# The first projection unit makes values, queries and keys together, and the squares of x leave GpSimd

## The chip, the cores and the metric

The kernel runs on one core of one Trainium2 chip. The metric is the device time of one execution in microseconds (us). The core has five engines, each with a queue of its own that is worked off in a fixed order: TensorE (PE, matmuls; PEld is its weight loads), VectorE (DVE), ScalarE (ACT), GpSimd (POOL) and SyncE (SP), which here only starts the DMAs. Waits between engines go over semaphores.

## What is computed

One decoder layer on 256 positions of width 1024, all in fp32:

```
hn  = rmsnorm(h, g_attn[i])
qkv = hn @ w_in[i]                       # (256, 3072)
qa, ka, va = split_heads(qkv[..., :1536], 8)
qb, kb, vb = split_heads(qkv[..., 1536:], 8)
ya = rmsnorm(merge_heads(dilated_mixture(qa, ka, va, slopes_a)), g_out_a[i])
yb = rmsnorm(merge_heads(moba_attention(qb, kb, vb, slopes_b)), g_out_b[i])
h = h + concat([ya, yb]) @ w_out[i]
hn = rmsnorm(h, g_mlp[i])
h = h + square(relu(hn @ w_up[i])) @ w_down[i]
gate = sigmoid(rmsnorm(h, g_ple[i]) @ w_ple_gate[i] + b_ple_gate[i])
h = h + gate * (p[i] @ w_ple_proj[i])
out = rmsnorm(h, g_final)
```

At 256 positions both attentions become plain causal attention with a bias table per head (a distance penalty; in group A also the logarithm of how many of the three dilated branches see a key).

## The kernel before

Every fp32 matrix product is made of three matmuls in a rounded format: the function `mm3` (L151 to L155) multiplies high by high, high by low and low by high halves. So every weight slab and x itself are first split: ScalarE rounds the tile to its high half (`hi`, L75, or `xhi`, L219) and VectorE subtracts to get the low half (`lo`, L76, or `xlo`, L220). x is kept transposed, as eight row blocks of 128 features by 256 tokens. The norm of x is not applied ahead of the projection but behind it: the squares of x are summed (`xsq`, L245 to L254), a matmul with ones gives the sums per token (`x_stats`), and the reciprocal root scales values (`v_evac`), queries and keys (`evac_qk`, by way of `x_bcast`, which spreads it over the partitions as `rb`).

The work is a list of units. A unit has slabs of weights (1 MB each, four row blocks by 512 columns) and a generator of steps; one step is one `mm3`. `run_units` (L109) loads the slabs two units ahead, splits the next unit's slabs in pieces while the steps of this unit run, and calls the functions that the unit's table `inserts` names after a given number of steps. The units of the projection are: values of group A (16 steps of two times 512 columns' worth of tokens by columns), then queries and keys of head pairs 0 and 1 (32 steps of 256 columns), of pairs 2 and 3, the same two for group B, and values of group B. The attention of a head pair is cut into functions that are inserted there: `E_` scales q and k and splits them, `B_` builds the bias on GpSimd, `S_` makes the scores, their softmax and, on GpSimd at L337, the normalised probabilities `pb`, `T_` transposes `pb` on TensorE (L347), `V_` multiplies with the values. With two bias buffers, `B_` of a pair waits until the scores of the pair two ahead have read theirs; on GpSimd it stands ahead of the `pb` steps of the pair before.

The first unit is special. Its loads are cut into single row blocks of 128x512 (256 KB; the first one in halves), with x between them, in groups of blocks `(0, 1), (1, 2), (2, 4), (4, 6), (6, 8)`; the first block of x comes with the gains in one tensor `head` (147 KB). All of its splitting, and the squares on GpSimd, are issued ahead of its matmuls:

```
for k0, k1 in groups:
    if k0 == 0:
        x_split(k0, k1)
        ...
    else:
        ps[k0]()
        x_split(k0, k1)
    for k in range(k0 + 1, k1):
        ps[k]()
    x_squares(k0, k1)
```

The rest of the kernel (output projection, MLP, gate, final norm) follows as further units.

## Time and profile before

| | us |
|---|---|
| timed runs | 351.67, 349.98, 351.51; median 351.51 |
| the profiled execution | 348.54 |
| its span, first to last instruction | 346.8 |
| PE busy | 331.6 (96%) |
| DVE busy | 221.6 (64%) |
| ACT busy | 198.3 (57%) |
| POOL busy | 91.0 (26%) |
| mean granted clock of TensorE | 0.989 |

The profiled execution is one run, 1.7 us longer than its span, and 3.0 us shorter than the median of the timed ones. The busy share of an engine is a mean over the whole span. TensorE has two clock levels, 1.2 and 2.4 GHz; the granted clock of a stretch is the mean share of the higher one. The ends of matmuls in a profile are modelled; their starts are recorded.

### The profile page before, as it was taken

The numbers are of one execution on the slowest core, as the hardware profiler recorded it, in microseconds if no ns is written. First come the engines' busy times: TensorE is split into PE (matmuls) and PEld (weight loads), VectorE is DVE, ScalarE is ACT, GpSimd is POOL, SyncE is SP. The second block draws the span as 40 slices with busy tenths as digits, with TensorE's granted clock in tenths as the row PEclk, the third lists the DMA queues.
The fourth block names the chain that finished last, engine by engine and source line by source line (L and its number), as shares of the span: only waits on it lengthen the run. The fifth ranks groups of instructions, "written<-read, shape, count | busy, mean of one in ns | idle before, by whom it ended". The sixth has DMA issues, their size and how long they took to land.

```text
span 346.8 us, 5629 instructions
## 1 busy us (share of the span) xinstructions
PE 331.6 (96%) x2188; PEld 296.6 (86%) x2188; DVE 221.6 (64%) x371; ACT 198.3 (57%) x370; POOL 91.0 (26%) x120
## 2 busy tenths in 40 slices
PE   7899999999989999999999999999999999999990
PEld 6689889999866889898998988989989899888890
DVE  4898999786855669637537275293553843757563
ACT  5676667785783668738345374372652825458431
POOL 1887574554222001311010110110201102000443
PEclk9899999999999999999999999999999999999997
DMA  6996844435264078563737618356194472700011
GB/s 180 370 381 227 316 160 135 159 123 194 94 241 154 15 241 315 200 231 106 259 124 239 246 38 327 124 169 259 58 322 163 133 246 107 242 2 0 2 61 61
DMA packets 10827, 60.87 MB, mean 176 GB/s; under 512 B 1200, under 2 KB 1968, under 8 KB 4016
## 3 DMA queue, kind: packets, MB, share of 16 engines
q1 hardware_dynamic: 10800, 60.51, 49.5%
q8 instruction: 17, 0.28, 0.3%
q14 instruction: 10, 0.08, 0.1%
HBM read 59.46 MB, written 1.05 MB: 174 GB/s over the span
## 4 chain that ended last, share of the span: by engine, by line
PE 81%; POOL 7%; DVE 5%; ACT 2%; issue 2%; DMA 2%; SPq 1%; POOLq 0%; DVEq 0%; ACTq 0%
PE ps L153 26%; PE ps L154 25%; PE ps L155 25%; DVE lo L76 3%; POOL xsq L254 2%; POOL pb L337 2%; DMA xT<-in_xT 2%; POOL sq L253 1%; PE ps L359 1%; PE ps L316 1%; PE ps L347 1%; ACT pb L331 1%; PE ps L476 1%; PE ps L360 1%; SPq L212 0%
## 5 line engine op out<-in xcount | busy, mean ns | idle before, releaser
L76 DVE SCALAR_TENSOR_TENSOR lo<-raw,head,hi 128x512 fp32r<-128x512 f32 (+2 forms) x137 | 109.8, 851 | 24.3 <-ACT hi L75 24.2
L75 ACT ACTIVATE hi<-raw,head 128x512 fp32r<-128x512 f32 (+2 forms) x137 | 92.6, 734 | 26.0 <-PE ps L154 11.2
L153 PE MATMUL ps<-hhi,hi 128*128 128x256 f32 x256 | 72.6, 283 | 0.0
L155 PE MATMUL ps<-hhi,lo 128*128 128x256 f32 x256 | 72.4, 283 | 0.0
L154 PE MATMUL ps<-hlo,hi 128*128 128x256 f32 x256 | 72.4, 283 | 0.0
L84 DVE TENSOR_TENSOR lo<-raw,hi 128x1024 fp32r<-128x1024 f32 x34 | 41.5, 1254 | 28.1 <-ACT hi L83 28.0
L540 POOL TENSOR_TENSOR sq<-r 128x512 f32<-128x512 f32 (+1 forms) x18 | 19.9, 1107 | 141.8 <-ACT r L538 141.8
L153 PE MATMUL ps<-hi,u 128*128 128x512 f32 x128 | 50.2, 392 | 0.0
L83 ACT ACTIVATE hi<-raw 128x1024 fp32r<-128x1024 f32 x34 | 34.3, 1052 | 27.2 <-PE ps L155 25.5
L154 PE MATMUL ps<-lo,u 128*128 128x512 f32 x128 | 49.9, 390 | 0.0
L155 PE MATMUL ps<-hi,u 128*128 128x512 f32 x128 | 49.8, 389 | 0.0
L153 PEld LDWEIGHTS ps<-hhi,hi 128*128 128x128 f32 x256 | 49.1, 192 | 0.3
L154 PEld LDWEIGHTS ps<-hlo,hi 128*128 128x128 f32 x256 | 49.1, 192 | 0.3
L155 PEld LDWEIGHTS ps<-hhi,lo 128*128 128x128 f32 x256 | 49.1, 192 | 0.0
L153 PE MATMUL ps<-xhi,hi 128*128 128x256 f32 x128 | 37.8, 297 | 0.0
L154 PE MATMUL ps<-xlo,hi 128*128 128x256 f32 x128 | 36.0, 282 | 0.0
L155 PE MATMUL ps<-xhi,lo 128*128 128x256 f32 x128 | 35.4, 282 | 0.0
L543 DVE TENSOR_TENSOR u<-sq,u 128x512 fp32r<-128x512 f32 (+1 forms) x18 | 11.7, 651 | 34.0 <-ACT u L542 34.0
L155 PEld LDWEIGHTS ps<-hi,u 128*128 128x128 f32 x128 | 24.0, 188 | 5.0
L153 PEld LDWEIGHTS ps<-hi,u 128*128 128x128 f32 x128 | 24.1, 188 | 4.7
L154 PEld LDWEIGHTS ps<-lo,u 128*128 128x128 f32 x128 | 24.1, 188 | 4.7
L153 PEld LDWEIGHTS ps<-xhi,hi 128*128 128x128 f32 x128 | 24.4, 191 | 1.2 <-issue 0.7
(128 smaller groups left out, 540.2 us busy)
## 6 DMA issues: line engine op xcount, KB each, us to landing
raw<-in_w_up SPq DMA_DIRECT2D x16, 1024.0 KB, 5.0
raw<-in_w_down SPq DMA_DIRECT2D x16, 1024.0 KB, 4.8
raw<-in_w_in SPq DMA_DIRECT2D x10, 1024.0 KB, 6.3
raw<-in_w_out SPq DMA_DIRECT2D x4, 1024.0 KB, 4.8
raw<-in_w_gate SPq DMA_DIRECT2D x4, 1024.0 KB, 4.9
raw<-in_w_in SPq DMA_DIRECT2D x7, 256.0 KB, 6.7
h_sb<-in_x SPq DMA_DIRECT2D x1, 1024.0 KB, 7.2
raw<-in_w_ple SPq DMA_DIRECT2D x1, 1024.0 KB, 4.9
```

What stands on the lines that cost most here:

```text
L75: nc.scalar.activation(h, r, AF.Copy, scale=sc)
L76: nc.vector.scalar_tensor_tensor(l, r, sc, h.bitcast(F32), op0=ALU.mult, op1=ALU.subtract)
L83: nc.scalar.activation(h, r, AF.Copy)
L84: nc.vector.tensor_tensor(l, r, h.bitcast(F32), op=ALU.subtract)
L153: nc.tensor.matmul(ps, lhs[0], rhs[0], start=start, stop=False)
L154: nc.tensor.matmul(ps, lhs[0], rhs[1], start=False, stop=False)
L155: last_mm[0] = nc.tensor.matmul(ps, lhs[1], rhs[0], start=False, stop=stop)
L253: nc.gpsimd.tensor_tensor(sq, x, x, op=ALU.mult)
L254: nc.gpsimd.tensor_tensor(xsq, xsq, sq, op=ALU.add)
L337: nc.gpsimd.tensor_scalar(pb[:, h, sl], pb[:, h, sl], nm[:, 2, c], 1.0, op0=ALU.mult, op1=ALU.mult)
L540: nc.gpsimd.tensor_tensor(sq, r, r, op=ALU.mult)
L543: nc.vector.tensor_tensor(o[1], sq, o[0].bitcast(F32), op=ALU.subtract)
```

## The change

The first unit now makes the values of group A and the queries and keys of head pairs 0 and 1, one row block of x after the other: for each block two steps of values, then four of q/k. It holds six accumulators at once. The loads are put in the order in which the blocks need them. The next unit's pieces begin after 33 of its 48 steps (`idle`). The squares of x are made on ScalarE and added on VectorE, and the scaled identity of `x_stats` is made on VectorE. The tables of inserts are rewritten: q and k of both pairs are finished at the end of the first unit and the start of the next, and scores, transposes and values of the later pairs move against the steps. The diff, cut to its core:

```diff
@@ run_units
-        ps = [p for s in units[0].slabs for p in s.pieces()]
-        for k0, k1 in groups:
...
+        v, qk = ([p for s in slabs_in[u] for p in s.pieces()] for u in range(2))
+        for k in range(KT):
+            if k in (0, 1, 2, 4):
+                x_split(k, k + (1 if k < 2 else 2))
+            for col in halves if k == 0 else [slice(None)]:
+                v[k](cols=col)
+            qk[k]()
+            if k == 4:
+                x_split(6, 8)
+            if k:
+                x_squares({1: range(2), 2: range(2, 4), 4: range(4, 6), 5: range(6, 8)}.get(k, ()))
...
-                want = min(len(todo), math.ceil(len(todo) * (j + 1) / (0.8 * u.n)))
+                want = min(len(todo), math.ceil(len(todo) * max(j + 1 - u.idle, 0) / (0.8 * (u.n - u.idle))))
@@ loads
+    for col in halves:
+        block_load(0, 0, 1, col)
+    block_load(1, 0, 1)
+    x_load(1, 2)
+    for u in range(2):
+        block_load(u, 1, 2)
+    x_load(2, 4)
+    for k in (2, 3):
+        for u in range(2):
+            block_load(u, k, k + 1)
+    x_load(4, 8)
+    for k in (4, 6):
+        for u in range(2):
+            block_load(u, k, k + 2)
@@ first_loads
-        slabs_in[1][0].load()
         nc.sync.dma_start(ident, a["consts"][:, 3 * S :])
-        slabs_in[1][1].load()
+        slabs_in[2][0].load()
         nc.sync.dma_start(consts[:, : 2 * S], a["consts"][:, : 2 * S])
+        slabs_in[2][1].load()
@@ x_squares
-                nc.gpsimd.tensor_tensor(sq, x, x, op=ALU.mult)
-                nc.gpsimd.tensor_tensor(xsq, xsq, sq, op=ALU.add)
+                nc.scalar.activation(sq, x, AF.Square)
+                nc.vector.tensor_tensor(xsq, xsq, sq, op=ALU.add)
@@ x_stats
-            nc.gpsimd.tensor_scalar(diag[:, t], ident, xr["r"][:, t : t + 1], 1.0, op0=ALU.mult, op1=ALU.mult)
+            iv = nc.vector.tensor_scalar(diag[:, t], ident, xr["r"][:, t : t + 1], None, op0=ALU.mult)
@@ the new first unit, and two lines of its table and the next one's
+    def first_steps():
+        tiles = []
+        for k in range(KT):
...
+                for t in range(2):
+                    v_step(0, 0, k, t)
+                    yield
+            s = slabs_in[1][k // 4]
+            for c in range(4):
...
+                mm3(tiles[c][:, :S], (s.hi[:, k % 4, col], s.lo[:, k % 4, col]), (aT[0][:, k], aT[1][:, k]),
+                    k == 0, k == KT - 1)
...
+                yield
...
+             {33: [x_stats], 42: [x_bcast], 46: [VE(0), B_(0, 0)], 48: [E_(0, 0)]}, 60, 33),
...
+             {3: [E_(0, 1)], 8: [S_(0, 0), B_(0, 1), late_loads], 16: [E_(0, 2)], 22: [S_(0, 1), B_(0, 2)],
+              24: [T_(0, 0)], 30: [V_(0, 0)]}, 32),
```

The first place where instructions stand anew is ScalarE at the start of the program. In the names, `raw_111` and `raw_112` are the values' two slabs, `raw_113` and `raw_114` the q/k slabs of the first two pairs (before, `raw_138` and `raw_141`), `xT_108` is x. Before, the rows from the first high half on were:

```order
L219 ACTIVATE xhi_109<-head_67 128x256
L75 ACTIVATE hi_146<-raw_111,head_67 128x256 x2
L75 ACTIVATE hi_146<-raw_111,head_67 128x512
L219 ACTIVATE xhi_109<-xT_108 128x256
L75 ACTIVATE hi_146<-raw_111,head_67 128x512
L219 ACTIVATE xhi_109<-xT_108 128x512
L75 ACTIVATE hi_146<-raw_111,head_67 128x512
L75 ACTIVATE hi_172<-raw_112,head_67 128x512
```

Now the same place reads:

```order
L230 ACTIVATE xhi_109<-head_67 128x256
L261 ACTIVATE xsq_138<-head_67 128x256
L75 ACTIVATE hi_151<-raw_111,head_67 128x256 x2
L75 ACTIVATE hi_157<-raw_113,head_67 128x512
L230 ACTIVATE xhi_109<-xT_108 128x256
L264 ACTIVATE sq_168<-xT_108 128x256
L75 ACTIVATE hi_151<-raw_111,head_67 128x512
L75 ACTIVATE hi_157<-raw_113,head_67 128x512
L230 ACTIVATE xhi_109<-xT_108 128x512
L264 ACTIVATE sq_177<-xT_108 128x256
L75 ACTIVATE hi_151<-raw_111,head_67 128x512
```

Values and q/k blocks alternate, and a square stands behind each high half of x.

The second place is VectorE from q and k of pair 0 to the scores of pair 0 (the operations at L322 and L325, now L334 and L337, two for each head). Before:

```order
L287 TENSOR_TENSOR q_361<-ps4_283,rb_132 128x256
L288 SCALAR_TENSOR_TENSOR k_362<-ps5_291,rb_132 128x256
L76 SCALAR_TENSOR_TENSOR lo_288<-raw_198,head_67,hi_287 128x512 x4
L292 TENSOR_TENSOR q_366<-q_361,q_365 128x256
L294 TENSOR_TENSOR k_368<-k_362,k_367 128x256
L76 SCALAR_TENSOR_TENSOR lo_349<-raw_200,head_67,hi_348 128x512 x4
L287 TENSOR_TENSOR q_473<-ps8_378,rb_132 128x256
L322 ISA sc_445,nm_447<-ps10_431,bias_373 128x256
```

Now:

```order
L299 TENSOR_TENSOR q_419<-ps4_242,rb_137 128x256
L300 SCALAR_TENSOR_TENSOR k_420<-ps5_246,rb_137 128x256
L299 TENSOR_TENSOR q_454<-ps6_250,rb_137 128x256
L76 SCALAR_TENSOR_TENSOR lo_395<-raw_147,head_67,hi_394 128x512 x2
L304 TENSOR_TENSOR q_424<-q_419,q_423 128x256
L306 TENSOR_TENSOR k_426<-k_420,k_425 128x256
L76 SCALAR_TENSOR_TENSOR lo_395<-raw_147,head_67,hi_394 128x512 x2
L76 SCALAR_TENSOR_TENSOR lo_444<-raw_223,head_67,hi_443 128x512
L300 SCALAR_TENSOR_TENSOR k_455<-ps7_254,rb_137 128x256
L304 TENSOR_TENSOR q_459<-q_454,q_458 128x256
L334 ISA sc_499,nm_501<-ps12_485,bias_406 128x256
```

q and k of pair 1 (`q_454`, `k_455`) have come between those of pair 0 and the first scores; the low halves between are five instead of eight, and two more follow between the two heads' scores.

## Rows read from the trace of the kernel before

**Rows 1.** The page's part 1, TensorE: busy us, share, instructions.

```profile
PE 331.6 (96%) x2188; PEld 296.6 (86%) x2188; DVE 221.6 (64%) x371; ACT 198.3 (57%) x370; POOL 91.0 (26%) x120
```

**Rows 2.** Waits of TensorE, 0 to 55 us: us in total, times, longest.

```profile
PE ps L153 <- ACT xhi L219: 2.4, 2, 1.8
PE ps L347 <- POOL pb L337: 1.5, 2, 1.1
...
PE ps L260 <- POOL xsq L254: 0.8, 1, 0.8
```

**Rows 3.** The same from 56 to 110 us.

```profile
PE ps L347 <- POOL pb L337: 1.2, 1, 1.2
```

**Rows 4.** Stretches: us, busy (count) of each engine, granted clock, DMA share, GB/s.

```profile
6.00:8.00 2.00, 1.40 (x7) 1.05 (x6) 1.35 (x2) 1.09 (x2) 0.85 (x1) 1.00 0.68 173
...
10.00:12.00 2.00, 1.77 (x6) 1.17 (x7) 1.88 (x2) 1.54 (x3) 1.92 (x4) 0.90 0.90 281
12.00:14.00 2.00, 2.00 (x6) 1.52 (x5) 2.00 (x3) 1.63 (x3) 2.00 (x3) 0.50 1.11 434
14.00:16.00 2.00, 2.00 (x8) 1.62 (x7) 2.00 (x3) 1.70 (x3) 1.92 (x2) 0.75 0.98 405
```

**Rows 5.** Timeline of ScalarE, 2 to 20 us: start, us, operation [idle before].

```profile
5.11 0.72 ACT L75 ACTIVATE hi<-raw,head 128x512 fp32r<-128x512 f32 x1 [0.68 <-DMA raw<-in_w_in]
6.20 0.42 ACT L219 ACTIVATE xhi<-xT 128x256 fp32r<-128x256 f32 x1 [0.36 <-DMA xT<-in_xT]
7.33 0.73 ACT L75 ACTIVATE hi<-raw,head 128x512 fp32r<-128x512 f32 x1 [0.71 <-DMA raw<-in_w_in]
9.46 0.63 ACT L219 ACTIVATE xhi<-xT 128x512 fp32r<-128x512 f32 x1 [1.41 <-DMA xT<-in_xT]
...
11.20 0.72 ACT L75 ACTIVATE hi<-raw,head 128x512 fp32r<-128x512 f32 x1 [0.28 <-DMA raw<-in_w_in]
12.33 0.63 ACT L219 ACTIVATE xhi<-xT 128x512 fp32r<-128x512 f32 x1 [0.40 <-DMA xT<-in_xT]
...
17.57 2.56 ACT L75 ACTIVATE hi<-raw,head 128x512 fp32r<-128x512 f32 x4 [1.83 <-DMA raw<-in_w_in]
```

**Rows 6.** Timeline of VectorE, 3 to 36 us.

```profile
14.46 2.36 DVE L76 SCALAR_TENSOR_TENSOR lo<-raw,head,hi 128x512 fp32r<-128x512 f32 x2
...
28.44 0.42 DVE L287 TENSOR_TENSOR q<-ps,rb 128x256 f32<-128x256 f32 x1 [0.65 <-PE ps L155]
...
33.77 2.73 DVE L76 SCALAR_TENSOR_TENSOR lo<-raw,head,hi 128x512 fp32r<-128x512 f32 x4
```

**Rows 7.** Timeline of TensorE: two paces, first scores, first transposes.

```profile
19.74 0.39 PE L153 MATMUL ps<-hi,xhi 128*128 128x512 f32 x1
...
19.97 0.39 PE L154 MATMUL ps<-lo,xhi 128*128 128x512 f32 x1
...
34.09 0.91 PE L316 MATMUL ps<-k,q 64*128 64x256 f32 x12
...
35.26 0.28 PE L155 MATMUL ps<-xhi,lo 128*128 128x256 f32 x1
35.38 0.28 PE L153 MATMUL ps<-xhi,hi 128*128 128x256 f32 x1
...
44.04 0.55 PE L347 MATMUL ps<-ident,pb 128*128 128x128 f32 x3 [1.11 <-POOL pb L337]
```

**Rows 8.** Timeline of GpSimd, 26 to 46 us.

```profile
38.02 0.94 POOL L304 TENSOR_SCALAR bias<-consts 128x256 f32<-128x256 f32 x2 [4.80 <-DVE nm L325]
...
40.65 3.34 POOL L337 TENSOR_SCALAR pb<-pb,nm 128x256 f32<-128x256 f32 x4
```

**Rows 9.** Groups of GpSimd, 2 to 30 us: count, busy us, mean ns.

```profile
L254 POOL TENSOR_TENSOR xsq<-xsq,sq 128x256 f32<-128x256 f32 x7 | 7.3, 1049 | 0.3
```

**Rows 10.** Groups of VectorE, 30 to 110 us.

```profile
L322 DVE CUSTOM_DVE_ANT_0 sc<-ps,bias 128x256 f32<-128x256 f32 x16 | 6.7, 417 | 3.0 <-PE ps L316 2.9
L325 DVE CUSTOM_DVE_ANT_0 sc<-ps,bias 128x128 f32<-128x128 f32 x16 | 4.5, 283 | 0.0
```

More of the change, by code (lines that the diff above doesn't have):

```diff
@@ L88, in block_kernel, with __init__ @@
     class Unit:
-        def __init__(self, slabs, steps, inserts=None, n=None):
-            self.slabs, self.steps, self.inserts, self.n = slabs, steps, inserts or {}, n
+        def __init__(self, slabs, steps, inserts=None, n=None, idle=0):
+            self.slabs, self.steps, self.inserts, self.n, self.idle = slabs, steps, inserts or {}, n, idle
     later = []
@@ L110, in run_units @@
         first_loads()
[L111 to L122 removed]
+        v, qk = ([p for s in slabs_in[u] for p in s.pieces()] for u in range(2))
[9 more added lines that the diff above has]
+                x_squares({1: range(2), 2: range(2, 4), 4: range(4, 6), 5: range(6, 8)}.get(k, ()))
         for i, u in enumerate(units):
[L124 to L126 removed]
+            for s in units[i + 2].slabs if i + 2 < len(units) else []:
+                s.load()
             todo = [p for s in (units[i + 1].slabs if i + 1 < len(units) else []) for p in s.pieces()]
@@ L406, in v_evac, with v_step @@
         for t in range(2):
-            nc.scalar.activation(vt[g][:, t], held[g][t], AF.Copy, scale=xr["r"][:, t : t + 1])
+            ia = nc.scalar.activation(vt[g][:, t], held[g][t], AF.Copy, scale=xr["r"][:, t : t + 1])
+        first.append(ia)
+    def v_step(u, g, k, t):
+        if k == t == 0:
+            vt[g] = ap.tile([P, 2, 512], F32, tag="vt", name="vt", bufs=2)
+            held[g] = [bank() for _ in range(2)]
+        s = slabs_in[u][k // 4]
+        tok = slice(t * P, (t + 1) * P)
+        mm3(held[g][t], (aT[0][:, k, tok], aT[1][:, k, tok]), (s.hi[:, k % 4], s.lo[:, k % 4]),
+            k == 0, k == KT - 1)
@@ L409, in v_steps @@
     def v_steps(u, g):
         def steps():
-            vt[g] = ap.tile([P, 2, 512], F32, tag="vt", name="vt", bufs=2)
-            ps = [bank() for _ in range(2)]
             for k in range(KT):
-                s = slabs_in[u][k // 4]
-                parts = halves if u == 0 and k == 0 else [slice(0, 512)]
-                for col in parts:
+                for t in range(2):
+                    v_step(u, g, k, t)
+                    yield
+        return steps
+    def first_steps():
+        tiles = []
+        for k in range(KT):
+            if k == 0:
+                vt[0] = ap.tile([P, 2, 512], F32, tag="vt", name="vt", bufs=2)
+                held[0] = [bank() for _ in range(2)]
+                s = slabs_in[0][0]
+                for col in halves:
@@ L417, in steps @@
                     for t in range(2):
                         tok = slice(t * P, (t + 1) * P)
-                        mm3(ps[t][:, col], (aT[0][:, k, tok], aT[1][:, k, tok]),
-                            (s.hi[:, k % 4, col], s.lo[:, k % 4, col]), k == 0 and col == parts[0], k == KT - 1)
-                        if col == parts[-1]:
-                            yield
-            held[g] = ps
-        return steps
+                        mm3(held[0][t][:, col], (aT[0][:, 0, tok], aT[1][:, 0, tok]),
+                            (s.hi[:, 0, col], s.lo[:, 0, col]), not col.start, False)
@@ new lines, in first_steps @@
+                yield
+                yield
+            else:
+                for t in range(2):
+                    v_step(0, 0, k, t)
+                    yield
+            s = slabs_in[1][k // 4]
+            for c in range(4):
+                if k == 0:
+                    tiles.append(bank())
+                col = slice(c * P, (c + 1) * P)
+                mm3(tiles[c][:, :S], (s.hi[:, k % 4, col], s.lo[:, k % 4, col]), (aT[0][:, k], aT[1][:, k]),
+                    k == 0, k == KT - 1)
+                if k == KT - 1 and c % 2:
+                    qk_ps[0, c // 2] = tiles[c - 1], tiles[c]
+                yield
```

54 lines of the change are left out of this document (17 added, 37 removed).

## The prediction, on record before the run

> **What bounds the kernel now.** I read the busy shares first. TensorE is busy for 331.6 of the 346.8 us of the span [rows 1], so only time in which TensorE stands or runs slowly can be won, and the change issues the same projection matmuls as before. Then I read what TensorE waited for. In the first 55 us it waited 2.4 us for the high halves of x, 1.5 us for the normalised probabilities `pb` and 0.8 us for `xsq`, the sum of squares [rows 2]; later, up to 110 us, there is one wait worth naming, 1.2 us, again for `pb` [rows 3]. The stage table adds a loss that no wait shows: the granted clock is 0.90, 0.50 and 0.75 in the three stretches from 10 to 16 us [rows 4], so 0.4, 2.0 and 1.0 us passed at 1.2 GHz instead of 2.4, which halves 3.4 us of work and costs 1.7 us. Before it fell TensorE had been busy for 1.40 us of the 2 us from 6 to 8 [rows 4] and had then stood for 1.8 us at a stretch [rows 2]. So the place is the front of the kernel: 2.4 + 1.7 + 0.8 us in the two units that the change merges, and 1.5 us at the first transposes.
>
> **The paces.** A dense 512-column matmul starts every 0.23 us, a 256-column one every 0.12 us [rows 7]. A row block of x is 6 of the first kind for the values (1.37 us) and 12 of the second for two head pairs (1.44), together 2.81 us; eight of them are 22.5 us. ScalarE makes a high half of 128x512 in 0.72 us, or every 0.61 us back to back (2.56 us for 4), and a 128x256 pass in 0.42 (0.36 back to back) [rows 5]. VectorE makes a low half in 1.18 us while GpSimd works on squares, and in 0.68 while GpSimd stands still [rows 6]: 33.77 lies in a gap of GpSimd, which begins its next work at 38.02 [rows 8].
>
> **Arrivals.** ScalarE's starts after a DMA wait tell when each place of the queue has landed. Counting bytes in the queue's order, 671 KB are there at 5.1, 1065 at 7.3, 1327 at 9.4, 1851 at 11.2, 2113 at 12.3 and 4211 at 17.5 us [rows 5]; the last stretch is 400 KB per us. The new queue has other tensors at the same places and begins with seven DMAs of the same sizes. So I take the same clock for the same byte. Then the first block of q/k weights is there at 5.1, values block 1 at 7.3, q/k block 1 at 9.4, x blocks 2 and 3 at 10.3, values block 2 at 11.2, q/k block 2 at 12.3, block 3 by 13.6, x blocks 4 to 7 at 14.9, the rest between 16.2 and 20.1, the next unit's two slabs at 22.9 and 26.2.
>
> **The first unit, block by block.** Each block waits for landing + 0.73 (high half) and then + 0.75 (low half).
> Values block 0: the square of x now stands between the high half of x and that of the weights on ScalarE, so it starts 0.3 us later, at 4.4, and ends at 6.1. Q/k block 0 runs at once, to 7.5. Values block 1: high half 8.05, so 0.55 us idle; low half 8.84, another 0.35; ends 9.8. Q/k block 1: high half 10.2, low half 11.0, 0.4 and 0.55 idle; ends 12.2. Values block 2: low half 12.7, 0.3 idle; ends 13.9. From there the halves are ready before TensorE is: block 3's q/k low half at 15.2 against 16.7, values block 4's at 18.3 against 18.4. Five blocks and a half at 2.81, plus 0.6 us each for the two small statistics steps, end the unit at **30.6**. Idle sum: 2.2 us, in pieces of up to 0.55, so I let the clock stay at 2.4 GHz.
> VectorE has in this unit 16 low halves (0.68), x's low halves (about 3.2 in all) and seven new additions, which I price at 0.41 each as the 128x256 operations that read q at 28.44 [rows 6]: 17 us. ScalarE has 16 x 0.61, x (about 2.4) and 8 squares at 0.36 to 0.42: 15.5. Both fit under 22.5, so the moved squares cost 0.3 us at the start and nothing after. On GpSimd seven additions at 1.05 us and as many squares disappear [rows 9], with the 0.8 us wait for `xsq`. The two scalings of the identity that move to VectorE cost it under 0.4 each, between low halves that are not needed before 30.6; the constants' and x's late DMAs move by one place in SP's queue and are waited for by nobody in the trace: nothing.
> Before, the same 48 + 96 matmuls end at 35.38, with the first scores (about 1.0 us with their change of form) among them [rows 7]: 34.4 without. So the unit is **3.8 us** shorter. Bounds: 2.2 us more if everything arrives in time, down to 2 us less if the landings lag by a microsecond and the clock falls.
>
> **What happens to it at the first transposes.** The gain passes on only if the first attention chain moves up too. In the old unit the first pair's q and k are finished in the middle (q read at 28.44), now all four finish in the last block, at 29.5 to 30.5, and both engines stand before that, since in their fixed order the value evacuations are ahead of the next unit's second slab on ScalarE and q of pair 0 is ahead of it on VectorE. From 30.7 ScalarE has, in its new order, 2 high halves, q, k, 2 high halves, q, one high half, k, 2 high halves: 7 x 0.61 + 4 x 0.36, and 1.1 us of waiting for k of pair 1 on VectorE. That ends at 37.6. VectorE's two low halves, the later one done at 38.4, stand ahead of the second head's score reductions (0.42 + 0.28, a little overlapped [rows 10]), which end at 39.0. GpSimd, as before, first builds the bias of pair 2, whose buffer these reductions free: 2.6 us, then 3.4 us for the four `pb` steps [rows 8], to **45.1**. Check by the old chain: from q at 28.44 to the end of `pb` at 43.99 are 15.6 us; from q at 29.9 that gives 45.5.
> TensorE is there earlier: 30.6 + 24 steps of 0.36 + two sets of scores 2.1 = 41.3, so it waits about 2.1 us for the first head and 1.3 for the second, 3.4 where it now loses about 1.9 (the 1.5 of [rows 2] and the ends that the waits don't count). The second head's transposes start at 45.1, against 44.04 now [rows 7]. But then 17 steps of that slab are left, now only 8; 9 steps are 3.2 us. So at this point 44.0 + 3.2 - 45.1 = **2.2 us** are won: 3.8 less 1.5 given back.
>
> **Later.** Between the first and the last transposes no wait for `pb` shows [rows 2, 3], at 16 to 19 steps from scores to transposes; the new table has 14 to 17, and the pair that loses most loses five steps, 1.8 us, with other inserts between. I cost these at nothing, bounds 0 and 1.8. In the last unit the 1.2 us wait [rows 3] should lose about 0.4: the scores of the pair ahead stand 3 steps earlier, so ScalarE is free sooner for the last q and k. The bounds are 0 and 1.2. The MLP is not touched.
>
> **Sum.** 2.2 + 0.4 = **2.6 us**, 348.5 to 345.9 us for the profiled execution. That execution is 3.0 us under the median of the timed runs, 351.5; with the same difference I predict **348.9 us**.
>
> **Rivals.**
> The clock falls again. For it: 2.2 us of idle pieces lie between 7.5 and 12.7. Against: the old fall came after 1.8 us in one piece, and none of these is over 0.55. It costs up to 1.7 us: gain 0.9, 350.6.
> The chain is short enough that the transposes don't wait. The 3.4 us come back: gain 6.0, 345.5. It needs `pb` by 41.6, 13 us after q where 15.6 are on record.
> The chain is longer. If VectorE's 7 low halves in it run beside GpSimd at 1.18 instead of 0.68, it grows by up to 3.5 us. For it: the bias of pairs 0 and 1 must be built. Against: their tables land by about 23.5 and GpSimd has nothing else then. Half of the price: gain 0.9, 350.6.
> Arrivals decide, and the kernel is slower. The unit needs 640 KB per row block where the old one needed 384. The slowest stretch, 671 KB to 1327 KB between 5.1 and 9.4, ran at 150 KB per us. If that pace lasted to the end of the small pieces (2.64 MB), q/k block 3 would land at 18.3 instead of 13.6, and values block 4 start at 23.0 instead of 18.1: 4.8 us lost, 2.2 slower, 353.7. It becomes slower from a mean of some 160 KB per us on. Against it: from 12 to 14 us pieces of the same size move at 434 [rows 4]. The Trainium skill (DMA: Bandwidth & Descriptors, Bandwidth) speaks for it: it wants transfers of at least 1 MiB for three quarters of the peak, and this change cuts two such loads into smaller ones; by that rule the small pieces stay slow and this rival holds. The 434 of the stretch above disagrees.
> The squares don't free VectorE: low halves stay at 1.18. Then a block costs VectorE 2 x 1.18 + 0.6 + 0.5 = 3.4 us against 2.81, the unit ends some 5 us later, and the kernel takes about 353.9.
>
> **How the numbers follow.** Forecast 0.45 (347.5 to 350); clock 0.17; no wait 0.12; longer chain 0.14; arrivals 0.09; VectorE stays slow 0.03. The range leaves out the last two and some of the no-wait case: 345.5 to 352.3. About 0.5% (1.8 us) is what a measurement of this kernel tells from no change. Most of the forecast, the no-wait case and a little of the two milder rivals are faster by more: 0.56; the last two and a tail of the long chain slower: 0.12; the rest 0.32.
>
> **What would show it.** Low halves of 0.66 to 0.75 us in the first 20 us; the last matmul of the first unit near 30.6 (plus or minus 1); idle pieces under 0.6 us and a granted clock of 1.00 from 10 to 16; no wait for `xsq`; a wait of about 3 us for `pb` at the first transposes, the largest of TensorE, with `pb` ending near 45.1; the last `pb` wait under 1.2. Wrong it is if q/k block 1 lands after 10.5, if the clock falls, or if `pb` ends before 43 or after 47.

## The result, and the profile after

| | before | after |
|---|---|---|
| timed runs, median (us) | 350.75 (349.51 to 351.67, 4 runs) | 347.07 (346.67 to 347.60, 4 runs) |
| ratio of the runs, 95% interval | | 0.9906 (0.988 to 0.9933) |
| the profiled execution (us) | 348.54 | 347.60 |
| its span (us) | 346.8 | 345.8 |
| PE, DVE, ACT, POOL busy (us) | 331.6, 221.6, 198.3, 91.0 | 333.2, 216.8, 199.8, 74.1 |

The change makes the kernel 0.9% faster, 3.3 us by the ratio. The two profiled executions show less: 348.54 to 347.60. The profile of before is of an execution shorter than all four of its timed runs, that of after is the longest of its four. So the profiles tell where time went in one execution each, and the runs how much was won.

The matmuls at L153 to L155 of before are at L151 to L153 now, the transposes at L359, the `pb` steps at L349, the biases at L316 and L318. First the busy line of the page, with [rows 1] before:

```profile
PE 333.2 (96%) x2188; PEld 298.9 (86%) x2188; DVE 216.8 (63%) x380; ACT 199.8 (58%) x378; POOL 74.1 (21%) x103
```

GpSimd has lost 16.9 us of work, VectorE 4.8, in spite of the additions that it took over, since its operations got shorter.

TensorE's waits from 0 to 55 us (in total, times, longest), where [rows 2] has those of before:

```profile
PE ps L359 <- POOL pb L349: 2.3, 2, 2.0
PE ps L151 <- ACT hi L75: 1.1, 1, 1.1
...
PE ps L152 <- DVE lo L76: 0.3, 1, 0.3
```

The wait for `xsq` is gone, those for x have become 1.1 and 0.3 us in one place, and the wait for `pb` is now the largest. From 55 to 110 us no wait is listed any more, so the 1.2 us of [rows 3] are gone as well.

The stage table answers [rows 4] (us, busy and count of PE, PEld, DVE, ACT, POOL, then granted clock, DMA share, GB/s):

```profile
6.00:8.00 2.00, 2.00 (x19) 2.00 (x18) 1.82 (x4) 1.35 (x3) 0.00 (x0) 1.00 0.87 208
10.00:12.00 2.00, 1.20 (x10) 0.99 (x9) 1.03 (x2) 1.36 (x3) 0.00 (x0) 1.00 1.02 368
12.00:14.00 2.00, 1.46 (x5) 1.01 (x6) 1.76 (x4) 2.00 (x5) 0.00 (x0) 1.00 1.05 425
14.00:16.00 2.00, 2.00 (x17) 1.87 (x16) 1.90 (x3) 1.60 (x4) 0.00 (x0) 1.00 1.02 414
42.00:44.00 2.00, 0.42 (x2) 0.42 (x3) 2.00 (x5) 0.66 (x2) 2.00 (x3) 0.84 1.03 365
44.00:46.00 2.00, 1.67 (x9) 1.27 (x8) 2.00 (x11) 1.56 (x7) 1.49 (x3) 0.50 0.31 127
46.00:48.00 2.00, 2.00 (x11) 2.00 (x11) 0.48 (x2) 0.68 (x3) 1.83 (x4) 0.50 0.65 139
48.00:50.00 2.00, 2.00 (x12) 1.59 (x12) 0.00 (x0) 0.00 (x0) 1.73 (x5) 0.50 0.92 377
50.00:52.00 2.00, 2.00 (x19) 1.74 (x16) 0.72 (x3) 0.58 (x2) 0.00 (x0) 0.95 0.05 21
```

The clock stays at 2.4 GHz from 6 to 16 us, but now it is 0.84, 0.50, 0.50, 0.50 and 0.95 from 42 to 52 us: 6.8 us at 1.2 GHz. The transposes stand just there. TensorE's timeline (start, us, operation, idle before):

```profile
41.29 0.28 PE L153 MATMUL ps<-xhi,lo 128*128 128x256 f32 x1
43.58 0.90 PE L359 MATMUL ps<-ident,pb 128*128 128x128 f32 x3 [2.01 <-POOL pb L349]
44.81 0.90 PE L359 MATMUL ps<-ident,pb 128*128 128x128 f32 x3 [0.33 <-POOL pb L349]
...
45.72 0.41 PE L152 MATMUL ps<-xlo,hi 128*128 128x256 f32 x1
45.94 0.41 PE L153 MATMUL ps<-xhi,lo 128*128 128x256 f32 x1
...
50.84 0.28 PE L152 MATMUL ps<-xlo,hi 128*128 128x256 f32 x1
50.95 0.29 PE L153 MATMUL ps<-xhi,lo 128*128 128x256 f32 x1
```

It stands for 2.01 us, transposes the first head, waits again, and then its 256-column matmuls start every 0.22 us (45.72, 45.94) until 50 us, where they should start every 0.12 (50.84, 50.95).

To see what each place is worth I add up, stretch by stretch, by how much the starts of TensorE's matmuls lie further apart than the usual 0.12 us (256 columns) and 0.23 (512 columns):

| us lost in | before | after | difference |
|---|---|---|---|
| 4 to 31 us (first unit of after) | 6.8 | 3.2 | -3.6 |
| 31 to 41 | 0.7 | 0.9 | +0.2 |
| 41 to 45.3 (first transposes) | 2.3 | 3.3 | +1.0 |
| 45.3 to 51 (half clock in after) | 0.5 | 2.5 | +2.0 |
| 51 to 93 | 3.7 | 4.7 | +1.0 |
| 93 to 101 (last `pb` wait of before) | 1.7 | 0.1 | -1.6 |
| from 101 | 1.6 | 1.6 | 0 |

Of 5.2 us won, 4.2 are given back: 3.0 at the first transposes and behind them, 1.2 in small pieces from 31 to 41 and from 51 to 93 us. The stretches hold slightly different work in the two kernels, and which gaps are counted as lost moves single entries by up to 0.6 us (in the last row by more, in both kernels alike), so the small entries are rough; the sum of the last column, -1.0, is the difference of the spans.

### The profile page after: what moved, and what is told of

Read it like the earlier page. It is cut to its first block, busy times and chain, and to the rows that moved or that the text cites. A ratio compares the mean times of both kernels' runs of the same rounds, so it can differ in the third digit from the quotient of the medians.

```text
span 345.8 us, 5641 instructions
## 1 busy us (share of the span) xinstructions
PE 333.2 (96%) x2188; PEld 298.9 (86%) x2188; DVE 216.8 (63%) x380; ACT 199.8 (58%) x378; POOL 74.1 (21%) x103
## 3 DMA queue, kind: packets, MB, share of 16 engines
HBM read 59.46 MB, written 1.05 MB: 175 GB/s over the span
## 4 chain that ended last, share of the span: by engine, by line
PE 92%; DMA 2%; POOL 2%; DVE 1%; SPq 1%; ACT 0%; issue 0%; POOLq 0%; DVEq 0%
PE ps L151 29%; PE ps L152 28%; PE ps L153 28%; DMA raw<-in_w_in 2%; PE ps L328 2%; PE ps L371 2%; PE ps L359 2%; PE ps L519 1%; POOL pb L349 1%; SPq L208 1%; PE ps L372 1%; POOL bias L318 1%; DVE lo L76 0%; POOL bias L316 0%; PE ps L271 0%
## 5 line engine op out<-in xcount | busy, mean ns | idle before, releaser
L76 DVE SCALAR_TENSOR_TENSOR lo<-raw,head,hi 128x512 fp32r<-128x512 f32 (+2 forms) x137 | 105.0, 813 | 24.9 <-ACT hi L75 24.6
L151 PE MATMUL ps<-hhi,hi 128*128 128x256 f32 x256 | 72.6, 283 | 0.0
L153 PE MATMUL ps<-hhi,lo 128*128 128x256 f32 x256 | 72.5, 283 | 0.0
L151 PE MATMUL ps<-hi,u 128*128 128x512 f32 x128 | 50.2, 392 | 0.0
L153 PE MATMUL ps<-hi,u 128*128 128x512 f32 x128 | 49.8, 389 | 0.0
L151 PEld LDWEIGHTS ps<-hhi,hi 128*128 128x128 f32 x256 | 49.1, 192 | 0.3
L153 PEld LDWEIGHTS ps<-hhi,lo 128*128 128x128 f32 x256 | 49.1, 192 | 0.0
L151 PE MATMUL ps<-xhi,hi 128*128 128x256 f32 x128 | 38.7, 303 | 0.0
L152 PE MATMUL ps<-xlo,hi 128*128 128x256 f32 x128 | 36.9, 289 | 0.0
L153 PE MATMUL ps<-xhi,lo 128*128 128x256 f32 x128 | 36.7, 289 | 0.0
L586 DVE TENSOR_TENSOR u<-sq,u 128x512 fp32r<-128x512 f32 (+1 forms) x18 | 11.7, 650 | 34.0 <-ACT u L585 34.0
L153 PEld LDWEIGHTS ps<-hi,u 128*128 128x128 f32 x128 | 24.0, 188 | 5.1
L151 PEld LDWEIGHTS ps<-hi,u 128*128 128x128 f32 x128 | 24.1, 188 | 4.7
L151 PEld LDWEIGHTS ps<-xhi,hi 128*128 128x128 f32 x128 | 25.2, 197 | 1.5 <-issue 0.7
```

Of the source, the lines that this page charges most:

```text
L76: nc.vector.scalar_tensor_tensor(l, r, sc, h.bitcast(F32), op0=ALU.mult, op1=ALU.subtract)
L151: nc.tensor.matmul(ps, lhs[0], rhs[0], start=start, stop=False)
L152: nc.tensor.matmul(ps, lhs[0], rhs[1], start=False, stop=False)
L153: last_mm[0] = nc.tensor.matmul(ps, lhs[1], rhs[0], start=False, stop=stop)
L586: nc.vector.tensor_tensor(o[1], sq, o[0].bitcast(F32), op=ALU.subtract)
```

## The experiments

Two questions stay after this reading. Which part of the change brings the gain, the merged unit or the squares? And what does the wait at the first transposes cost, with the half clock behind it? Each ratio is to runs of the kernel before on the same chip, whose median there was 349.2 to 350.0 us; kernels are compared with each other by these ratios.

### The wait at the first transposes

First the changed kernel once more, as a base.

> The changed kernel once more, as the base of the three kernels that run beside it. Both theories: 346.7 to 347.6 us, with the wait for pb at the first transposes of 2 to 3 us, and after it a stretch at half clock that is there in some executions and shorter in others.

346.02 us (343.97 to 347.66), ratio 0.9905 (0.987 to 0.9939). Its profile waits 2.7 us for `pb` and has half the stretch of half clock. The mean clock of its six executions and their times go together: 0.982 with 347.66, 0.990 to 0.991 with 345.94 to 346.65, 0.995 with 343.97.

Then three ways of taking the wait away. The transposes later:

```diff
-              24: [T_(0, 0)], 30: [V_(0, 0)]}, 32),
+              30: [T_(0, 0)]}, 32),
...
-             {0: [E_(0, 3)], 5: [S_(0, 2), B_(0, 3)], 7: [T_(0, 1)], ...
+             {0: [E_(0, 3)], 4: [V_(0, 0)], 5: [S_(0, 2), B_(0, 3)], 7: [T_(0, 1)], ...
```

> The changed kernel with the transposes of pair 0 six steps later (step 30 instead of 24) and its values in the next unit. Theory: TensorE stands there only because pb comes late, and nothing else is late behind it. The first head then waits 0 and the second up to 0.9 us instead of 2.2 and 0.6; and since TensorE no longer stands for 2 us, its clock stays at 2.4 GHz there, which saves up to 2.4 us more in an execution where it fell for 6.8 us. 345.1 us if the clock falls as before, 343.5 if it does not. Rival 1: the wait is only moved, because values and scores of the next pairs come later by it: 347. Rival 2: the clock falls there whether TensorE waits or not: 345.1 with a stretch at half clock near 43 to 50 us.

343.97 us (343.6 to 344.15), ratio 0.9843 (0.982 to 0.9867). `pb` is waited for 1.2 us in two pieces, 0.7 the longer, and the clock is 1.00 there. The interval lies below that of the changed kernel on the same chip (from 0.987 on), if only just.

The order on GpSimd, where the bias of pair 2 was built ahead of `pb` of pair 0 (the `issue_after` holds it behind the last `pb` step, kept in `pr[0, 0]["n"]`):

```diff
...
+    def after_pb():
+        with tc.issue_after(pr[0, 0]["n"].ins):
+            make_bias(0, 2)
+
-    B_ = lambda g, j: (lambda: make_bias(g, j))
+    B_ = lambda g, j: after_pb if (g, j) == (0, 2) else (lambda: make_bias(g, j))
```

> The changed kernel with one change of order on GpSimd: the bias of pair 2 stands behind the four pb steps of pair 0 instead of ahead of them. Theory (the prediction's chain): the bias holds pb back. pb then starts with the reciprocal at about 39.9 instead of 41.9 us, is finished at 43.0 instead of 44.75, and TensorE waits 0.4 and 0.8 us instead of 2.2 and 0.6: 1.6 us less, 345.5 us; less again if the clock stays up. Rival: pb is held by the exponentials on ScalarE or by VectorE sharing with GpSimd, and ends after 44: gain under 0.7 us, 346.5 to 347.

344.08 us (343.71 to 344.5), ratio 0.9849 (0.9825 to 0.9873). GpSimd's timeline, first of the changed kernel, then of this one:

```profile
38.70 1.21 POOL L316 TENSOR_SCALAR bias<-consts 128x256 f32<-128x256 f32 x2 [7.39 <-DVE nm L337]
39.99 1.88 POOL L318 TENSOR_TENSOR bias<-bias,consts 128x256 f32<-128x256 f32 x2
41.87 2.89 POOL L349 TENSOR_SCALAR pb<-pb,nm 128x256 f32<-128x256 f32 x4
```

```profile
40.39 2.90 POOL L349 TENSOR_SCALAR pb<-pb,nm 128x256 f32<-128x256 f32 x4 [8.69 <-DVE nm L345]
43.37 1.21 POOL L316 TENSOR_SCALAR bias<-consts 128x256 f32<-128x256 f32 x2
44.66 1.87 POOL L318 TENSOR_TENSOR bias<-bias,consts 128x256 f32<-128x256 f32 x2
```

In the changed kernel the bias takes from 38.70 to 41.87, and `pb` of four steps ends at 44.75. With the order turned, `pb` starts at 40.39 and ends 1.5 us earlier. One wait of 0.8 us for `pb` is left.

Both edits, with the transposes at step 28 and the values at step 2 of the next unit:

> Both: pb of pair 0 ahead of the bias of pair 2 on GpSimd, and the transposes of pair 0 at step 28 (values at step 2 of the next unit). Theory: no wait for pb at all at the first transposes, no stretch at half clock there: 2.8 us and up to 2.4 us less than the changed kernel, 342.5 to 344.3 us. Rival (the wait is only moved): a new wait of 1 to 2 us for pb or for the bias of pair 2 in the next unit, 346 us. Rival (the clock falls anyway): 344.3 with a half-clock stretch.

344.21 us (343.07 to 345.06), ratio 0.9852 (0.9827 to 0.9877): no better than either alone. The first transposes no longer wait, but the values of pair 0 wait 0.8 us for the copied transposes, since they follow too soon, and the transposes of pair 1 wait 0.7 for their `pb`, which now stands behind two biases. The rival of the moved wait holds for the part beyond one edit.

That three different edits end at the same time asks whether they gain by the wait or by the clock. So a kernel in which TensorE is kept busy during the wait, but waits all the same:

```diff
             ps = bank()
+            for _ in range(9 if (g, j, h) == (0, 0, 0) else 0):
+                nc.tensor.matmul(ps, aT[0][:, 0, :P], slabs_in[2][0].hi[:, 0], start=True, stop=True)
```

> The changed kernel with nine matmuls of 512 columns, whose result nobody reads, issued just ahead of the first transposes of pair 0; they fill 2.0 us of the 2.2 us in which TensorE otherwise stands, and the transposes come no earlier. Theory: TensorE's clock falls at 43 us because TensorE stood before it; with the filler there is no half-clock stretch between 40 and 55 us, the wait itself still costs its 2.8 us, and the time is that of the changed kernel less what the fall costs, 344.0 to 345.2 us in every execution. Rival: the fall has another cause (a rhythm in time, or the transposes): half clock there all the same, 346 us with the same spread.

345.0 us (344.02 to 345.72), ratio 0.9868 (0.9836 to 0.99). Its stage table:

```profile
42.00:44.00 2.00, 1.32 (x7) 0.65 (x7) 2.00 (x9) 0.50 (x2) 1.81 (x3) 1.00 0.82 340
44.00:46.00 2.00, 2.00 (x18) 2.00 (x18) 1.50 (x7) 1.72 (x9) 1.52 (x3) 1.00 0.22 70
```

The clock is 1.00 throughout, from 46 to 48 us too, and the mean clock of its five executions is 0.992 to 0.994. So it is the standing by which the clock falls here. The fall alone costs some 1.3 us (0.9868 against 0.9905). The intervals overlap, so the size is uncertain; the profile's 2.0 us for a fall of 6.8 and its place agree, and the six executions of the changed kernel above lie 2.2 us apart between the one at 0.995 and those near 0.990. What is left for the wait itself is 0.7 (0.9849 against 0.9868), less than the 1.5 us by which it shrinks in the profile; these two intervals overlap nearly whole, so that a part for the wait is not shown.

### Squares and merged unit apart

The squares alone, in the kernel before:

```diff
-                nc.gpsimd.tensor_tensor(xsq, x, x, op=ALU.mult)
+                nc.scalar.activation(xsq, x, AF.Square)
...
-                nc.gpsimd.tensor_tensor(sq, x, x, op=ALU.mult)
-                nc.gpsimd.tensor_tensor(xsq, xsq, sq, op=ALU.add)
+                nc.scalar.activation(sq, x, AF.Square)
+                nc.vector.tensor_tensor(xsq, xsq, sq, op=ALU.add)
...
-            nc.gpsimd.tensor_scalar(diag[:, t], ident, xr["r"][:, t : t + 1], 1.0, op0=ALU.mult, op1=ALU.mult)
+            nc.vector.tensor_scalar(diag[:, t], ident, xr["r"][:, t : t + 1], None, op0=ALU.mult)
```

> The kernel before, with only the squares of x (and the scaled identity of x_stats) moved from GpSimd to ScalarE and VectorE; units, loads and inserts as before. Theory (the first unit of before is bound by landings and by TensorE's clock, and VectorE has room): the low halves there fall from 1.18 to 0.7 us, the 0.8 us wait for xsq goes, nothing else moves: 0.8 to 1.2 us less than the kernel before, about 348.2 where that takes 349.2. Rival: half of the whole gain or more is the squares, since faster low halves also shorten the 2.4 us wait and keep the clock up: 346.5 to 347.5. Rival: a square of 0.36 us ahead of a high half on ScalarE delays it where TensorE waits: no gain, 349.2.

346.65 us (345.56 to 347.62), ratio 0.9912 (0.9882 to 0.9941). That is as much as the whole change gains; the theory's 0.8 to 1.2 us falls. The time is that of the second theory, but its reasons are not what the profile shows. The wait for the high halves of x is no shorter and the clock falls all the same (0.74, 0.50 and 0.91 in the three stretches from 10 to 16 us):

```profile
PE ps L153 <- ACT xhi L219: 2.6, 1, 2.6
```

```profile
12.00:14.00 2.00, 2.00 (x6) 1.52 (x6) 2.00 (x5) 2.00 (x5) 0.00 (x0) 0.50 1.09 432
```

The clock has a price in this kernel. Of its six executions three have a mean clock of 0.990 to 0.991, as the profiled one, and take 347.3 to 347.6 us; the other three, at 0.994 to 0.995, take 345.6 to 346.1, some 1.6 us less.

The merged unit alone, with the squares back on GpSimd:

```diff
-                nc.scalar.activation(xsq, x, AF.Square)
+                nc.gpsimd.tensor_tensor(xsq, x, x, op=ALU.mult)
...
-                nc.scalar.activation(sq, x, AF.Square)
-                nc.vector.tensor_tensor(xsq, xsq, sq, op=ALU.add)
+                nc.gpsimd.tensor_tensor(sq, x, x, op=ALU.mult)
+                nc.gpsimd.tensor_tensor(xsq, xsq, sq, op=ALU.add)
```

> The changed kernel with the squares of x and their sum back on GpSimd (merged unit, loads and inserts as in the changed kernel). Prediction's rival of slow low halves: 1.18 us each, so VectorE needs about 3 us per row block against TensorE's 2.81 and the sum of squares, 15 operations at 1.05 us behind x's last landing at 14.7 us, comes about when x_stats wants it: the unit ends 1 to 5 us later, 347.5 to 351. Rival: the merged unit is bound by landings up to 13 us and has room after, so that VectorE's slower low halves are hidden: within 0.5 us of the changed kernel, 346.0 to 346.5.

349.01 us (347.81 to 350.26), ratio 0.9979 (0.9959 to 1.0). VectorE's timeline of it, then of the changed kernel:

```profile
14.96 2.12 DVE L231 TENSOR_TENSOR xlo<-xT,xhi 128x512 fp32r<-128x512 f32 x2
17.00 7.36 DVE L76 SCALAR_TENSOR_TENSOR lo<-raw,head,hi 128x512 fp32r<-128x512 f32 x7
```

```profile
13.24 2.07 DVE L76 SCALAR_TENSOR_TENSOR lo<-raw,head,hi 128x512 fp32r<-128x512 f32 x3
```

Seven low halves take 7.36 us, 1.05 each, and GpSimd is busy beside them; without GpSimd three take 2.07, 0.69 each. TensorE's first unit ends only 0.3 us later (its last matmul starts at 30.95 instead of 30.62), but VectorE comes to q and k of pair 0 at 30.74 instead of 29.86, and TensorE waits longer at the transposes:

```profile
PE ps L359 <- POOL pb L349: 2.9, 2, 2.6
...
PE ps L152 <- DVE lo L76: 0.9, 2, 0.6
```

By the ratios the squares cost this kernel 2.6 us. The two profiled executions, both with 6.8 us of half clock, differ by 0.8 (348.37 and 347.60); where the rest lies these profiles don't show.

To see why the squares were worth so much, a second profile of the kernel before.

> The kernel before once more, for a second profile of it. Its runs spread from 348.1 to 351.2 us; the one profile at hand, 348.5, lies at the low end, and taken with it the squares moved alone show 1.3 us, while the medians show 3.3. Theory: in its usual runs TensorE waits longer for xsq than the 0.8 us of that profile, since GpSimd's squares run at varying speed beside VectorE: a wait for xsq of 1.5 us or more in a run of 349.5 or longer. Rival: the spread lies in the landings and in the clock (a longer wait for xhi, or a longer half-clock stretch), and the xsq wait stays under 1 us.

Its ten executions have a median of 350.02 us (348.66 to 351.93), and the profiled one is the shortest, 348.66, with a wait of 0.9 us for `xsq`. So neither theory on the long executions can be judged by it. It shows something else. Its stage table, against [rows 4]:

```profile
10.00:12.00 2.00, 1.68 (x6) 1.11 (x7) 1.64 (x2) 1.35 (x3) 1.92 (x3) 1.00 0.92 307
12.00:14.00 2.00, 2.00 (x10) 1.28 (x8) 2.00 (x3) 1.94 (x4) 2.00 (x3) 1.00 1.10 423
14.00:16.00 2.00, 1.62 (x8) 1.02 (x7) 2.00 (x3) 1.57 (x3) 1.92 (x3) 1.00 1.01 410
```

The clock did not fall here, and yet the execution is no shorter than that of [rows 4], with 1.7 us at stake by the prediction. Its timelines of VectorE and of GpSimd tell why:

```profile
11.60 2.03 DVE L76 SCALAR_TENSOR_TENSOR lo<-raw,head,hi 128x512 fp32r<-128x512 f32 x2
...
14.57 2.36 DVE L76 SCALAR_TENSOR_TENSOR lo<-raw,head,hi 128x512 fp32r<-128x512 f32 x2
...
17.88 5.54 DVE L76 SCALAR_TENSOR_TENSOR lo<-raw,head,hi 128x512 fp32r<-128x512 f32 x5
```

```profile
9.61 0.61 POOL L253 TENSOR_TENSOR sq<-xT 128x256 f32<-128x256 f32 x1 [3.14 <-DMA xT<-in_xT]
...
14.06 2.32 POOL L254 TENSOR_TENSOR xsq<-xsq,sq 128x256 f32<-128x256 f32 x2
...
18.52 2.08 POOL L253 TENSOR_TENSOR sq<-xT 128x256 f32<-128x256 f32 x2
20.56 2.32 POOL L254 TENSOR_TENSOR xsq<-xsq,sq 128x256 f32<-128x256 f32 x2
```

VectorE works without a gap from 11.6 to 23.4 us, at 1.0 to 1.2 us for a low half, and GpSimd without a gap beside it, at 1.05 to 1.19 us for an operation that takes 0.61 when VectorE stands (at 9.61). These two set the pace of the first unit here. At 2.4 GHz TensorE only waits for low halves instead: it loses 6.9 us from 4 to 31 us with the fast clock, 6.8 with the slow one.

But at half clock TensorE is just as slow, so neither limit goes without the other. VectorE reads q of pair 0 at 28.44 in [rows 6], with the half clock and the squares on GpSimd. In this second profile the half clock is gone; in that of the squares moved alone the squares are gone and the half clock is there; in the kernel of the next section, whose other edit acts only from 37 us on, both are gone. In this order:

```profile
28.56 0.42 DVE L287 TENSOR_TENSOR q<-ps,rb 128x256 f32<-128x256 f32 x1 [0.65 <-PE ps L155]
```

```profile
28.25 0.42 DVE L287 TENSOR_TENSOR q<-ps,rb 128x256 f32<-128x256 f32 x1
```

```profile
27.05 0.42 DVE L287 TENSOR_TENSOR q<-ps,rb 128x256 f32<-128x256 f32 x1
```

The matmul that waits for x blocks 2 and 3 starts at 10.14, 10.24, 10.56 and 10.39 us in the four profiles; from there to q are 18.3, 18.3, 17.7 and 16.7 us. Taking the half clock away gains nothing, taking the squares away 0.6 us, both 1.6.

These are four executions. Of the kernel before, 67 executions have their mean clock on record: 28 at 0.992 or more take 349.2 us on average, 23 at 0.987 to 0.990 (the profile of [rows 4] has 0.989) 349.8, 14 at 0.986 or less 350.7, and two lie between. So half clock goes with longer executions there too, 0.6 us for the middle group against 1.6 with the squares moved; the mean clock doesn't tell in which stretch it fell. And the profiled executions of before and of the squares moved alone differ by 1.3 us where the ratio says 3: the profiles place less than half of what the squares bring.

Whether the wait for `xsq` alone is what the squares' move takes away:

```diff
-             {4: [x_stats], 12: [x_bcast, VE(0)], 16: [E_(0, 0), B_(0, 0)], 31: [S_(0, 0), B_(0, 1)]}, 32),
+             {8: [x_stats], 14: [x_bcast, VE(0)], 16: [E_(0, 0), B_(0, 0)], 31: [S_(0, 0), B_(0, 1)]}, 32),
```

> The kernel before with x_stats four steps later (step 8 of the second unit instead of 4) and x_bcast two steps later (14 instead of 12); the squares stay on GpSimd. It takes 1.4 us of waiting for xsq away and leaves the slow low halves as they are. Theory (what the moved squares alone gain is the wait for xsq): most of the 3 us, 346.5 to 348 us. Rival (the gain is VectorE's, which GpSimd no longer slows): under 1 us, 349 us.

350.01 us (348.93 to 352.05), ratio 1.0005 (0.9987 to 1.0024): nothing. The profile doesn't wait for `xsq` any more, but it waits at the first scores:

```profile
PE ps L316 <- DVE k L294: 0.8, 1, 0.8
...
PE ps L155 <- DVE lo L76: 0.5, 2, 0.4
```

The wait has moved to the next product of VectorE, as it would where VectorE is late as a whole. But `x_bcast` moved too, which alone makes q and k later, so this is not a clean test; with the timelines above it speaks against the theory and for the rival.

### What the merged unit is worth

With the wait at the transposes out of the way in both:

```diff
 (the squares' diff above, and)
...
-    B_ = lambda g, j: (lambda: make_bias(g, j))
+    B_ = lambda g, j: after_pb if (g, j) == (0, 2) else (lambda: make_bias(g, j))
```

> The kernel before with the squares moved to ScalarE and VectorE and, on GpSimd, the bias of pair 2 behind the pb steps of pair 0: units, loads and inserts as before, so values first and no merged unit. It asks what the merged unit is worth once the wait at the first transposes is out of the way in both; its partner is the changed kernel with the same edit on GpSimd, 344.1 us. Theory: the merged unit wins the wait for the high halves of x (2.6 us at 7.5 to 10 us with the squares moved, against 1.2 us in the merged unit) and the half clock behind it, 1 to 2 us: this kernel takes 345.0 to 346.0 us, 1.6 to 0.6 less than the squares alone (346.65). Rival: the merged unit is worth nothing once the squares are moved: 344.1 us. Rival: the order on GpSimd matters only in the merged kernel: no gain over 346.65.

345.73 us (345.31 to 346.1), ratio 0.9899 (0.9882 to 0.9915), against 0.9849 (0.9825 to 0.9873) for the changed kernel with the same edit. The intervals don't meet: the merged unit, with the loads and the tables that come with it, is worth 0.5%, 1.7 us. Not all of it need be the unit's form: at the last transposes this kernel still waits 0.9 us for `pb`, the changed kernel with the same edit doesn't. The clock stays at 1.00 in this profile, so a fall that the theory counted on is not part of it. The kernel still waits for the high halves of x:

```profile
PE ps L153 <- ACT xhi L219: 2.0, 2, 1.1
...
PE ps L155 <- DVE lo L76: 0.5, 2, 0.4
```

Put together, as ratios to the kernel before:

| | old units | merged unit |
|---|---|---|
| squares on GpSimd | 1 | 0.9979 |
| squares on ScalarE and VectorE | 0.9912 | 0.9905 |
| the same, and `pb` of pair 0 ahead of the bias | 0.9899 | 0.9849 |

With the old units the order on GpSimd brings nothing that the intervals show (0.9912 to 0.9899); with the merged unit it is worth 0.6% (0.9905 to 0.9849, with intervals that just meet).

### The last wait, and a faster kernel

> The changed kernel with the scores of pair 2 of group B back at step 28 and the transposes of pair 1 at step 29 of the last q/k unit (now 25 and 27), as the kernel before had them. Theory of the prediction: it is these three steps that free ScalarE and GpSimd earlier for the last pair, so the wait for pb of 1.2 us at the last transposes comes back: 347.0 to 347.4 us. Rival: the wait went for another reason (the pieces and the other inserts stand differently): no wait over 0.4 us there, time as the changed kernel, 346.

```diff
-              20: [Y_(0)], 25: [S_(1, 2), B_(1, 3)], 27: [T_(1, 1)]}, 32),
+              20: [Y_(0)], 28: [S_(1, 2), B_(1, 3)], 29: [T_(1, 1)]}, 32),
```

346.98 us (345.58 to 347.88), ratio 0.9916 (0.9887 to 0.9946), and no wait for `pb` from 56 to 110 us. So it is not these three steps that took the 1.2 us of [rows 3] away. The two kernels with the old units and the squares moved still wait 0.9 us there; the rest of the new tables does it, and which line of them was not tried.

Last, all edits at once: the bias of pairs 2 and 3 behind `pb` of the pair two ahead, transposes of pair 0 at step 29, the values of pair 0 and the transposes and values of pair 1 at steps 4, 8 and 14 of the next unit, and x blocks 2 and 3 as two DMAs.

```diff
...
-    x_load(2, 4)
+    x_load(2, 3)
     for k in (2, 3):
         for u in range(2):
             block_load(u, k, k + 1)
+        if k == 2:
+            x_load(3, 4)
...
```

> The changed kernel with all at once: biases of pairs 2 and 3 behind the pb steps of the pair two ahead on GpSimd, transposes of pair 0 at step 29, values of pair 0 and the transposes and values of pair 1 one to four steps later, and x blocks 2 and 3 landing in two DMAs, block 3 two weight blocks later. Theory: no wait for pb over 0.3 us, no half-clock stretch, and the 0.9 to 1.1 us wait at 11 us shorter by the 128 KB that no longer stand ahead of values block 2, some 0.4 us: 1.3 us less than each of the three kernels with one of the edits (344.0), 342.7 us. Rival: the waits only move, or the landing does not follow the bytes ahead: 344.0.

342.52 us (342.19 to 342.61), ratio 0.9793 (0.9777 to 0.9809): faster than both kernels, by 7.2 us against before (0.0207 of 349.8). No wait for `pb` is left, and the clock doesn't fall:

```profile
PE ps L373 <- DVE pT L363: 1.7, 1, 1.7
PE ps L151 <- ACT hi L75: 1.1, 1, 1.1
```

A new wait of 1.7 us has come in, of the values of pair 1 for the copy of their transposes, which the new steps leave too little room; it is still to be had. The weight block is waited for at 6 us here (the first q/k block, not values block 2), so what the split of x brought by itself can't be told from this run.

## Why the prediction was right, and where it was not

The time, 347.07 us, lies between the forecast of 348.9 and the low end of the range, a little below the 347.5 to 350 that were given the largest chance, and faster by over 0.5% was the likeliest case. The kernel gained 3.3 us by the ratio where the sum said 2.6. The mechanisms agree only in part.

**Right: the arrivals.** ScalarE's starts after a DMA wait, against [rows 5]:

```profile
5.26 0.72 ACT L75 ACTIVATE hi<-raw,head 128x512 fp32r<-128x512 f32 x1 [0.74 <-DMA raw<-in_w_in]
...
8.18 0.72 ACT L75 ACTIVATE hi<-raw,head 128x512 fp32r<-128x512 f32 x1 [0.60 <-DMA raw<-in_w_in]
9.91 0.63 ACT L230 ACTIVATE xhi<-xT 128x512 fp32r<-128x512 f32 x1 [1.00 <-DMA xT<-in_xT]
...
11.49 0.72 ACT L75 ACTIVATE hi<-raw,head 128x512 fp32r<-128x512 f32 x1 [0.64 <-DMA raw<-in_w_in]
...
14.76 1.15 ACT L230 ACTIVATE xhi<-xT 128x512 fp32r<-128x512 f32 x2 [0.40 <-DMA xT<-in_xT]
```

"The same clock for the same byte" put q/k block 0, q/k block 1, x 2 and 3, values block 2 and x 4 to 7 at 5.1, 9.4, 10.3, 11.2 and 14.9 us. They came at 5.2, 8.2, 9.9, 11.5 and 14.7. The 8.2 is of this execution: from 6 to 8 us the loads ran at 208 GB/s here and at 229 to 342 in the seven other profiles with the same order. The pieces of 256 and 512 KB moved at 368 to 425 GB/s from 10 to 16 us, so the rival of slow arrivals fell. The rule of the Trainium skill (DMA: Bandwidth & Descriptors, Bandwidth) that speaks for loads of 1 MiB and more was no guide here: these pieces are a quarter and a half of that.

**Right: the first unit's end and the chain.** Forecast 30.6 us; the next unit's first matmul starts at 30.74. The low halves take 0.69 to 0.75 us up to 24 us. Of the attention chain the forecast had the score reductions done at 39.0, the bias behind them, and `pb` ending at 45.1: GpSimd begins the bias at 38.70 and ends `pb` at 44.75 (the bias takes 3.1 us where 2.6 were forecast, `pb` 2.9 where 3.4 were: two errors that cancel). TensorE comes to the transposes at 41.4 (forecast 41.3) and loses 2.8 us (forecast 3.4), the largest wait, as forecast. One reading of the prediction was wrong there: for the chain to keep TensorE from waiting, `pb` at 41.6 would have been 11.7 us after its q at 29.9, not 13, so that rival was further off than it says. Measured are 14.9.

**Right in part: the idle time of the unit.** 2.2 us in pieces of up to 0.55 were forecast, and pieces over 0.6 were to count against it. It is 1.1 and 0.3 us in one place, values block 2: q/k block 1 came 1.2 us earlier than forecast, so TensorE used up its work and stood once. The clock stayed up there, as forecast.

**Wrong: what bounded the kernel before.** The prediction took 1.7 us as lost to the half clock from 10 to 16 us, beside 2.4 us for x and 0.8 us for `xsq`, and gave the squares' move 0.8 us less 0.3 at the start. The profile without half clock loses the same from 4 to 31 us: VectorE and GpSimd were as slow as TensorE at half clock, and each limit hid the other. So the 1.7 us were not there to be won by the clock alone. [rows 6] held the sign of it, a low half of 1.18 us beside GpSimd and 0.68 without; the prediction used it only to ask whether VectorE fits under TensorE afterwards, not whether it did before. So the term of the squares was mis-sized: alone they bring 0.9%, some 3 us, of which the profiles place 1.3, and the merged unit brings nothing on top while the wait at the transposes stands. The other way round, the rival that low halves stay slow was priced at 5 us; with the squares back on GpSimd it cost 0.3 us at the unit's end and 2.6 in all. The Trainium skill (SBUF — State Buffer, Who interferes with whom) has the rule for the slow low halves: a VectorE instruction with two inputs in SBUF and a GpSimd instruction that reads SBUF shut each other out, and the one that comes second waits. The traces agree: the low half reads two tiles, and both sides grow, 0.69 to 1.05 and more on VectorE, 0.61 to 1.06 on GpSimd.

**Wrong: the rival of the falling clock was put at the wrong place.** It was looked for at 10 to 16 us, after the idle pieces of the first unit, and "if the clock falls" stood among the signs of being wrong. It came at 43.4 us, behind the wait of 2 us that the prediction itself had worked out and called the largest of TensorE. By the prediction's own remark on [rows 2] and [rows 4], that the old fall came behind a stand of 1.8 us, the new stand should have been given a chance of that price: 2.0 us in the profile, about 1.3 us in the runs. The sum had nothing for it.

**Mis-sized: the last unit.** 0.4 us was forecast of the 1.2 us wait; all of it went, and 1.6 us in that stretch. The reason given, scores three steps earlier, was not the cause; what was stays open.

**The sum and the offset.** In the profiles 3.6 us were won in the first unit where 3.8 were forecast, 3.0 were given back at the transposes where 1.5 were, 1.6 were won at the end where 0.4 were, and 1.2 were lost between, from 31 to 41 and from 51 to 93 us, where nothing was forecast: 1.0 us where the sum had 2.6. The medians moved by more than either. The 3.0 us between the profiled execution and the median of before did not carry over: the profile of after is 0.5 us above its median. So the forecast of 348.9 came near partly because an error in the offset and errors in the terms cancelled. What makes the executions of before spread over 348.0 to 351.9 us stays open: both of its profiles are of executions near 348.6, and the mean clock goes with about 1.5 us of it (the groups of 67 executions above).

## What to carry to other kernels

Before pricing a stall of TensorE, or a stretch at half clock, ask whether another engine works without a gap in that stretch; if it does, the two limits hide each other, and removing one of them gains little until the other goes as well (here nothing for the clock, 0.6 us for the squares, 1.6 for both). A gain at the front arrives at the next place where something else is late, so move the order there (here one bias behind `pb` on GpSimd, or the transposes by six steps) together with the change. And a wait of about 2 us on TensorE can have a second price behind it, the half clock.
